# Second half-step of an inference layer: the fourth operand sum, the left-over products and two fetches take other places in the order

## The chip, the cores and the metric

The kernel runs on one core of a Trainium2 chip. The metric is device time in microseconds (us) of one execution; a run's figure is one such time, and the median of the runs is compared. TensorE (PE) does matmuls out of the on-chip memory into accumulation banks; VectorE (DVE) and ScalarE (ACT) do elementwise work; GpSimd (POOL) and SyncE (SP) here mostly issue DMAs. Each engine works through its own instructions in order.

## The reference

One layer of a diffusion trunk for 512 latent and 128 context tokens (640 columns in the kernel): a SwiGLU half-step, a mixing of tokens, and a second SwiGLU half-step. Cut to what matters here:

```python
def swiglu(h, w1, w3, w2):
    return (jax.nn.silu(h @ w1) * (h @ w3)) @ w2

# layer(...)
hh = rmsnorm(x, g[0]) * (1 + m[1]) + m[0]
x = x + 0.5 * m[2] * swiglu(hh, p['ffn1_w1'][l], p['ffn1_w3'][l], p['ffn1_w2'][l])
...
hh = rmsnorm(x, g[2]) * (1 + m[7]) + m[6]
x = x + 0.5 * m[8] * swiglu(hh, p['ffn2_w1'][l], p['ffn2_w3'][l], p['ffn2_w2'][l])
```

All data are f32; the width is 1024, the hidden width 2816, that is 11 blocks of 256. `m` is the modulation, a product of the conditioning vector with a 1024 x 9216 matrix.

## The kernel before

**Number format.** A matmul reads f32 rounded to a shorter form (fp32r). So each operand is split: ACT copies it into a high part, DVE subtracts that from the original and writes a low part. A product is three matmuls: high by high, high by low, low by high. PE reads a weight's low part at every third matmul.

**Seven products for eight.** A half-step halves the 1024 rows (or the 4 blocks of a group) and the 640 tokens, and multiplies by a scheme with seven block products instead of eight. It needs four sums of operand quarters (S1 to S4 in `operand_sums`, line 349) and sums of weight quarters. One `Granule` (line 243) is one 1024 x 256 piece of a weight matrix, loaded into one of two buffers `raw`. `parts` (line 256) splits two quarters and a half quarter of it into wB and wC, and then forms three weight sums in place in `raw`; `sums` (line 282) splits the result into `ww`, 128x2048. wB serves products A11 and A12, wC S4, `ww` S1, S3, A22 and S2. Each product is 12 matmuls of 128x320.

**The loop.** `products` (line 425) runs over a list of granules. In each it puts the products into three banks X, Y and Z in this order: A11 into X, S1 into Z, the left-over A22 and, after S2, the left-over S4 of the granule before (`tail`), A12 into X, S3 into Y. ACT copies X into Y behind A11, and Y into u2 behind S2 and into u3 behind S3. The weights of the next granule are prepared meanwhile.

**Where it is used.** The first half-step (`HalfStep` with `n_plain` 11) uses the scheme for its up-projection only; its down-projection multiplies plainly, with w2 split by `Whole.split` (line 294). Beside that, `modulation` (line 888) lets DVE work off the modulation's columns, two reductions each, with `columns.tile(hs.at_vec)`, where `at_vec` names the DVE instruction behind which they are to be placed. The second half-step (`run`, line 596) has 20 granules in the up-projection (w1 and w3 of blocks 1 to 10; block 0 is done plainly ahead), then a down-projection over three groups of blocks: blocks 0 to 2 plainly in four column groups, then blocks 3 to 6 and 7 to 10 in 4 + 4 granules (`last`). The gated values go to DRAM (`g_dram`) and come back by `fetch` (line 608) as the operands of the down-projection.

**What sets the order.** A scheduler simulates the program and orders each engine's instructions; matmuls keep the written order. `tc.issue_after(i)` says that what follows comes behind instruction i. In `products`, `next_parts(copied, gr.low)` places the next granule's `parts` behind the copy of X and behind the low part of this granule's `ww`. In the second half-step the first two granules are special: the operand sums S1 to S4 are written as one chain on DVE ahead of the loop, S4's terms and low parts last, and the second granule's `parts` come behind the low part of S2 (`behind=summed`). The loads of x from `x2_dram` that follow overwrite the operands' source.

**Fetches.** Most fetches are issued on SP between weight loads; those for which a buffer is freed late are issued on POOL. In `used(i)` (line 634) two of the third group's seven, A11 and S1, go out on POOL behind S3 of `last[1]`; their buffers were last read by the plain products.

Of the kernel before, what the change touches and what calls it, by code (L numbers as in the profile page):

```python
# [7 lines left out]
F32 = mybir.dt.float32  # L8
# [15 lines left out]
FB = F // 256  # L24
# [7 lines left out]
def tile_trunk(ctx: ExitStack, tc: tile.TileContext, a: dict):  # L32
# [210 lines left out]
    class Granule:  # L243
# [5 lines left out]
        def load(self):  # L249
            self.raw = rawp.tile([128, 2048], F32, tag="raw", name="raw")[:, : 512 * self.nk].rearrange("p (k n) -> p k n", n=256)  # L250
            return self.fetch(self.raw)
# [4 lines left out]
        def parts(self, fp, ties=()):  # L256
            ties = iter(ties)

            def tied(*args):
                with ExitStack() as st:  # L260
                    t = next(ties, None)
                    if t is not None:
                        st.enter_context(tc.issue_after(t.ins))
                    tt(vec, *args)
# [17 lines left out]
        def sums(self):  # L282
# [3 lines left out]
            act(t[0], flat, AF.Copy)  # L286
# [4 lines left out]
    class Whole(Granule):  # L291


        def split(self, fp=None):
# [8 lines left out]
            for (c0, c1, h), (_, _, lw) in zip(*t):  # L303
                act(h, flat[:, c0:c1], AF.Copy)
                tt(vec, lw, flat[:, c0:c1], h.bitcast(F32), ALU.subtract)
# [8 lines left out]
    class HalfStep:  # L314
# [34 lines left out]
        def operand_sums(self, pair):  # L349
# [30 lines left out]
            for f, i, r in (  # L380
                (terms, S1, 0), (terms, S1, 1), (terms, S3, 0), (low, S1, 0), (terms, S2, 0), (low, S1, 1), (terms, S3, 1),
                (terms, S2, 1), (low, S2, 0), (low, S2, 1), (low, S3, 0), (low, S3, 1), (terms, S4, 0), (terms, S4, 1),
            ):
                f(i, r)
                if (f, i) == (low, S2):
                    behind = prev.ins
            low(S4, 0)
            low(S4, 1)
            return behind
# [35 lines left out]
        def products(self, work, between, then=(), behind=None, prepared=False, first=()):  # L425
# [11 lines left out]
            for i, (gr, A, done, used) in enumerate(work):  # L437
# [25 lines left out]
                if self.n_plain < FB and i:  # L463
                    next_parts(copied, gr.low)
# [3 lines left out]
                if tail:  # L468
                    tail[0]()
# [74 lines left out]
        def run_whole(self, x, gate, final, between, behind, first):  # L544
# [32 lines left out]
            for q in G:  # L577
                last = q == G[-1]
                for j in range(4):
# [3 lines left out]
                    if m + 1 < len(down):  # L583
                        down[m + 1].split(self.fp if last and j < 2 else None)
                    for hf in range(1 if last and j else 2):
# [10 lines left out]
        def run(self, x, gate, final, behind=None, first_ties=()):  # L596
# [19 lines left out]
            def between(i, at):  # L616
                if (i, at) == (0, 1):
# [7 lines left out]
            def down_done(q, j):  # L625
# [8 lines left out]
                def used(i):  # L634
                    if (q, j, i) == (1, 1, S3):
                        fetch(2, A11, nc.gpsimd)
                        fetch(2, S1, nc.gpsimd)
# [91 lines left out]
    with ExitStack() as ph:  # L729
# [134 lines left out]
        hs.operand_sums(lambda r: x_all[:, 2 * r : 2 * r + 2, :])  # L864
# [1138 lines left out]
    summed = hs.operand_sums(lambda r: x_pairs[r])  # L2003
    for g in range(4):
        nc.sync.dma_start(out=x_pairs[g], in_=x2_dram[:, 2 * g : 2 * g + 2, :])
    hs.run(
        lambda: x, half_m[:, 1], lambda d, hf: nc.sync.dma_start(out=a["y"][:, d, half(hf)], in_=x[d][:, half(hf)]),
        behind=summed, first_ties=[normed_last] * 5,
# [129 lines left out]
```

## Time and profile before

| | us |
|---|---|
| median of 3 runs (lowest to highest) | 1847.83 (1846.72 to 1850.73) |
| the profiled execution, own time | 1846.77 |
| its span, first to last instruction | 1845.0 |
| ACT busy | 841.9 (46%) |
| DMA, mean rate | 162 GB/s |

How to read it: a group or timeline row has the line of the kernel, the engine, the operation, then output<-inputs by the program's tile names. L39 is the helper of every elementwise operation of two tensors, L52 that of every matmul, so tiles tell more than lines. `ps_f` is an accumulation bank of the half-steps, `S` and `hm` are operands (hm holds the quarters of the modulated input, later fetched ones), `x` the operand's source, `raw`, `wB`, `wC` and `ww` weights, `u` a copy of a bank, `s` a gate, `g` a split gated value, `op` a fetched operand. In the timeline the first number is the start, the second the time until the row's last instruction ends, and the bracket the idle time before it with what ended it. Neighbouring instructions of an engine overlap by some 0.08 us. The up-projection of the second half-step begins at about 1411 us, its down-projection at about 1692.

### The profile page before, as it was taken

How to read it: one execution, taken by the hardware profiler on the slowest of the kernel's cores; microseconds unless marked ns; L12 is line 12 of the kernel's file. 1: busy time of each engine (PE TensorE's matmuls, PEld its weight loads, DVE VectorE, ACT ScalarE, POOL GpSimd, SP SyncE). 2: the span in 40 equal slices, each digit the busy share in tenths (PEclk: the TensorE clock that was granted, in tenths of full speed). 3: DMA queues.
4: the chain of work that ended last, by engine and by line, in shares of the span. 5: the costliest groups of instructions: out<-in, count | busy, mean ns of one | idle time of the engine just before them, and what ended most of it. 6: DMA issues, size and time to landing. Idle time of an engine off the chain costs nothing.

```text
span 1845.0 us, 30710 instructions
## 1 busy us (share of the span) xinstructions
PE 1801.0 (98%) x12658; PEld 1767.9 (96%) x12658; DVE 1292.5 (70%) x2173; ACT 841.9 (46%) x1447; POOL 34.9 (2%) x61
## 2 busy tenths in 40 slices
PE   6999999999999999999999999999999899999989
PEld 4999999999999999999999989999999899999989
DVE  6888886575786667854754557787767778886576
ACT  6654454112654453543543455673336455554232
POOL 0000001110000000000000000000000000000000
PEclk9999999999999999999999999999999999999999
DMA  8345448863323233221222254675652445557952
GB/s 333 138 154 171 153 150 321 319 222 125 119 79 132 74 106 116 88 99 52 81 102 75 95 171 130 216 249 208 211 183 75 154 149 169 191 165 278 351 206 85
DMA packets 125709, 299.75 MB, mean 162 GB/s; under 512 B 9473, under 2 KB 88705, under 8 KB 112897
## 3 DMA queue, kind: packets, MB, share of 16 engines
q1 hardware_dynamic: 116242, 257.09, 40.5%
q0 software_dynamic: 9328, 40.71, 6.1%
q8 instruction: 99, 1.62, 0.4%
q14 instruction: 40, 0.33, 0.1%
HBM read 234.20 MB, written 63.63 MB: 161 GB/s over the span
## 4 chain that ended last, share of the span: by engine, by line
PE 89%; DMA 4%; DVE 4%; ACT 2%; issue 1%; SPq 0%; DVEq 0%; ACTq 0%
PE ps_f L52 44%; PE ps_p L52 23%; PE ps_t L52 11%; PE sc L52 2%; PE ps_o L52 2%; PE ps_n L52 2%; DMA ada<-csil_dram 2%; DMA P<-nm_dram 1%; PE ps_wT L55 1%; PE ps_qkT L55 1%; PE ps_u L52 1%; DVE junk L712 1%; DMA x<-in_x 1%; DMA raw_a<-in_w_ada_k 1%; DMA raw_a<-in_w_ada_c 0%
## 5 line engine op out<-in xcount | busy, mean ns | idle before, releaser
L52 PE MATMUL ps_f<-S,ww 128*128 128x320 f32 x1992 | 320.0, 311 | 5.6 <-ACT ww L286 3.8
L52 PEld LDWEIGHTS ps_f<-S,ww 128*128 128x128 f32 x1992 | 300.7, 189 | 6.1 <-ACT ww L286 4.1
L52 PE MATMUL ps_p<-hH,wH 128*128 128x320 f32 x864 | 273.5, 316 | 1.0 <-DVE C L42 1.0
L52 PE MATMUL ps_p<-hH,wL 128*128 128x320 f32 x864 | 267.0, 309 | 0.0
L52 PE MATMUL ps_p<-hL,wH 128*128 128x320 f32 x864 | 266.8, 309 | 0.0
L52 PE MATMUL ps_f<-hm,ww 128*128 128x320 f32 x1248 | 200.2, 313 | 7.6 <-ACT ww L286 4.1
L52 PEld LDWEIGHTS ps_f<-hm,ww 128*128 128x128 f32 x1248 | 189.7, 191 | 8.8 <-ACT ww L286 4.4
L52 PE MATMUL ps_t<-wH,hH 128*128 128x256 f32 x640 | 185.4, 290 | 0.0
L52 PE MATMUL ps_t<-wH,hL 128*128 128x256 f32 x640 | 181.9, 284 | 1.1 <-DVE hL L39 1.1
L52 PE MATMUL ps_t<-wL,hH 128*128 128x256 f32 x640 | 181.6, 284 | 0.0
L39 DVE TENSOR_TENSOR ww<-raw,ww 128x2048 fp32r<-128x2048 f32 (+1 forms) x62 | 138.7, 2238 | 40.4 <-ACT ww L286 26.4
L52 PEld LDWEIGHTS ps_p<-hH,wH 128*128 128x128 f32 x864 | 162.4, 188 | 1.9 <-DVE C L42 1.4
L52 PEld LDWEIGHTS ps_p<-hL,wH 128*128 128x128 f32 x864 | 162.5, 188 | 0.5
L52 PEld LDWEIGHTS ps_p<-hH,wL 128*128 128x128 f32 x864 | 162.2, 188 | 0.0
L52 PE MATMUL ps_f<-hm,wB 128*128 128x320 f32 x1008 | 161.5, 309 | 0.0
L52 PEld LDWEIGHTS ps_f<-hm,wB 128*128 128x128 f32 x1008 | 151.3, 188 | 0.0
L39 DVE TENSOR_TENSOR wL<-raw,wH 128x2048 fp32r<-128x2048 f32 x49 | 112.1, 2288 | 40.5 <-ACT wH L122 40.4
L122 ACT ACTIVATE wH<-raw 128x2048 fp32r<-128x2048 f32 x49 | 93.6, 1910 | 80.8 <-PE ps_p L52 76.7
L286 ACT ACTIVATE ww<-raw 128x2048 fp32r<-128x2048 f32 x48 | 91.8, 1913 | 73.4 <-DVE raw L39 55.0
L39 DVE TENSOR_TENSOR raw<-raw 128x1024 f32<-128x1024 f32 x144 | 124.2, 863 | 1.4
L52 PEld LDWEIGHTS ps_t<-wH,hL 128*128 128x128 f32 x640 | 123.1, 192 | 1.5 <-DVE hL L39 1.5
L52 PEld LDWEIGHTS ps_t<-wL,hH 128*128 128x128 f32 x640 | 123.3, 193 | 0.2
(299 smaller groups left out, 3207.6 us busy)
## 6 DMA issues: line engine op xcount, KB each, us to landing
g_dram<-g SPq DMA_DIRECT2D x44, 640.0 KB, 4.6
raw_a<-in_w_ada_c SPq DMA_DIRECT2D x32, 512.0 KB, 3.9
raw<-in_w1b SPq DMA_DIRECT2D x11, 1024.0 KB, 4.9
raw<-in_w3b SPq DMA_DIRECT2D x11, 1024.0 KB, 7.1
raw<-in_w1a SPq DMA_DIRECT2D x10, 1024.0 KB, 4.7
raw<-in_w3a SPq DMA_DIRECT2D x10, 1024.0 KB, 4.8
hm<-g_dram POOLq DMA_DIRECT2D x8, 1280.0 KB, 10.5
raw_a<-in_w_ada_k SPq DMA_DIRECT2D x8, 1024.0 KB, 11.3
```

What stands on the lines that cost most here:

```text
L39: return eng.tensor_tensor(out=out, in0=in0, in1=in1, op=op)
L52: tc.keep_in_program_order(nc.tensor.matmul(*args, **kw))
L55: tc.keep_in_program_order(nc.tensor.transpose(*args, **kw))
L122: act(h, raw, AF.Copy)
L286: act(t[0], flat, AF.Copy)
L712: vec.tensor_tensor_reduce(out=junk, in0=raw, in1=self.csil[:, v, :], op0=ALU.mult, op1=ALU.add, scale=1.0, scalar=0.0, accum_out=mod[:, c ...
```

## The change

Five edits. (1) `operand_sums` no longer issues S4's terms and low parts itself, but gives back a function `last` that does; in the second half-step `run` calls it when the loop reaches its first granule, behind the last weight sum of the second granule, and the four x reloads follow it (`rest`). The first half-step calls it at once. (2) `next_parts` places the third and later granules' `parts` also behind ACT's high part of the current granule's `ww` (`gr.high`). (3) In the second granule of the up-projection the left-over A22 product comes ahead of S1. (4) The two fetches of `used(i)` go from POOL to SP, behind the load of `last[3]`. (5) In the first half-step's down-projection the modulation's reductions at the head of each step are placed behind the low part of the next w2 piece.

```diff
         def load(self):
...
-            return self.fetch(self.raw)
+            self.loaded = self.fetch(self.raw)
+            return self.loaded
...
-                    tt(vec, *args)
+                    self.at_vec = tt(vec, *args)
...
-            act(t[0], flat, AF.Copy)
+            self.high = act(t[0], flat, AF.Copy)
...
-                tt(vec, lw, flat[:, c0:c1], h.bitcast(F32), ALU.subtract)
+                self.low = tt(vec, lw, flat[:, c0:c1], h.bitcast(F32), ALU.subtract)
...
-                (terms, S2, 1), (low, S2, 0), (low, S2, 1), (low, S3, 0), (low, S3, 1), (terms, S4, 0), (terms, S4, 1),
+                (terms, S2, 1), (low, S2, 0), (low, S2, 1), (low, S3, 0), (low, S3, 1),
             ):
                 f(i, r)
-                if (f, i) == (low, S2):
-                    behind = prev.ins
-            low(S4, 0)
-            low(S4, 1)
-            return behind
+            behind = prev.ins
+
+            def last(ins=None):
+                nonlocal prev
+                prev = ins or prev
+                for f in (terms, low):
+                    for r in range(2):
+                        f(S4, r)
+
+            return behind, last
...
                 if self.n_plain < FB and i:
-                    next_parts(copied, gr.low)
+                    next_parts(copied, gr.low, gr.high)
+                early = tail and self.n_plain < FB and i == 1 and not prepared
+                if early:
+                    tail[0]()
                 into(Z, S1, True)
...
-                if tail:
+                if tail and not early:
                     tail[0]()
...
                         down[m + 1].split(self.fp if last and j < 2 else None)
+                        self.at_vec = down[m + 1].low
...
             def between(i, at):
+                if (i, at) == (0, 0):
+                    rest(work[1][0].at_vec)
...
                     if (q, j, i) == (1, 1, S3):
-                        fetch(2, A11, nc.gpsimd)
-                        fetch(2, S1, nc.gpsimd)
+                        with tc.issue_after(last[3][0].loaded):
+                            fetch(2, A11)
+                            fetch(2, S1)
...
-    summed = hs.operand_sums(lambda r: x_pairs[r])
-    for g in range(4):
-        nc.sync.dma_start(out=x_pairs[g], in_=x2_dram[:, 2 * g : 2 * g + 2, :])
+    summed, fourth = hs.operand_sums(lambda r: x_pairs[r])
+
+    def rest(ins):
+        fourth(ins)
+        for g in range(4):
+            nc.sync.dma_start(out=x_pairs[g], in_=x2_dram[:, 2 * g : 2 * g + 2, :])
```

What this does to the engines' orders is shown at three places. The numbers behind the names tell buffers apart; lines are those of each version.

**The second granule's weights on DVE and ACT** (raw_15053; x_14306 and x_14307 receive S4's terms, hm_14342 its split form). DVE before:

```order
L39 TENSOR_TENSOR S_15163<-x_13738,S_15163 128x640
L39 TENSOR_TENSOR x_14306<-x_14306,x_13737 128x2x320
L39 TENSOR_TENSOR x_14307<-x_14307,x_13738 128x2x320
L39 TENSOR_TENSOR wB_15210<-raw_15053,wB_15209 128x1024
L39 TENSOR_TENSOR wC_15212<-raw_15053,wC_15211 128x512
L39 TENSOR_TENSOR hm_14342<-x_14306,hm_14342 128x640
L39 TENSOR_TENSOR hm_14342<-x_14307,hm_14342 128x640
L39 TENSOR_TENSOR raw_15053<-raw_15053 128x2x4x128
L39 TENSOR_TENSOR s_15299<-ps_f_15222,u_15297 128x320
L39 TENSOR_TENSOR raw_15053<-raw_15053 128x4x128 x2
L39 TENSOR_TENSOR ww_15249<-raw_15053,ww_15248 128x2048
```

DVE now, at the same place:

```order
L39 TENSOR_TENSOR S_15163<-x_13738,S_15163 128x640
L39 TENSOR_TENSOR wB_15200<-raw_15053,wB_15199 128x1024
L39 TENSOR_TENSOR wC_15202<-raw_15053,wC_15201 128x512
L39 TENSOR_TENSOR raw_15053<-raw_15053 128x2x4x128
L39 TENSOR_TENSOR raw_15053<-raw_15053 128x4x128 x2
L39 TENSOR_TENSOR x_14306<-x_14306,x_13737 128x2x320
L39 TENSOR_TENSOR x_14307<-x_14307,x_13738 128x2x320
L39 TENSOR_TENSOR ww_15249<-raw_15053,ww_15248 128x2048
L39 TENSOR_TENSOR g_15280<-SO_14892,g_15280 128x1280
L39 TENSOR_TENSOR s_15299<-ps_f_15222,u_15297 128x320
L39 TENSOR_TENSOR hm_14342<-x_14306,hm_14342 128x640
L39 TENSOR_TENSOR hm_14342<-x_14307,hm_14342 128x640
```

The four instructions of S4 moved behind the weight sums, its low parts even behind `ww_15249`. ACT before, from the copy u3 of the first granule on (wB_15320 and ww_15357 are the third granule's):

```order
L422 ACTIVATE u_15297<-ps_f_15221 128x320
L516 ACTIVATE s_15299<-s_15299 128x320
L462 ACTIVATE ps_f_15305<-ps_f_15304 128x320
L271 ACTIVATE wB_15320<-raw_15207 128x1024
L271 ACTIVATE wC_15322<-raw_15207 128x512
L286 ACTIVATE ww_15248<-raw_15053 128x2048
L286 ACTIVATE ww_15357<-raw_15207 128x2048
L516 ACTIVATE s_15355<-ps_f_15221 128x320
L422 ACTIVATE u_15373<-ps_f_15305 128x320
L516 ACTIVATE s_15387<-s_15387 128x320
L422 ACTIVATE u_15416<-ps_f_15305 128x320
```

ACT now, from the second granule's high part on:

```order
L287 ACTIVATE ww_15248<-raw_15053 128x2048
L428 ACTIVATE u_15297<-ps_f_15221 128x320
L374 ACTIVATE hm_14342<-x_14306 128x640
L374 ACTIVATE hm_14342<-x_14307 128x640
L468 ACTIVATE ps_f_15305<-ps_f_15304 128x320
L272 ACTIVATE wB_15320<-raw_15197 128x1024
```

The high part moved ahead of u3, of the copy of X and of the third granule's wB and wC.

**The third granule's weights on ACT**, the rows that follow (raw_15197 was raw_15207 before; u_15373 and u_15416 are the second granule's u2 and u3):

```order
L272 ACTIVATE wC_15322<-raw_15197 128x512
L525 ACTIVATE s_15343<-ps_f_15221 128x320
L525 ACTIVATE s_15299<-s_15299 128x320
L428 ACTIVATE u_15373<-ps_f_15305 128x320
L525 ACTIVATE s_15387<-s_15387 128x320
L428 ACTIVATE u_15416<-ps_f_15305 128x320
L287 ACTIVATE ww_15357<-raw_15197 128x2048
L468 ACTIVATE ps_f_15424<-ps_f_15423 128x320
```

`ww_15357` stood right behind `ww_15248`; it now stands behind u_15416. From the fourth granule on `ww` stands ahead of the u3 of the granule before it, then and now.

**The third of the last eight granules on ACT** (raw_18088; raw_18168 is the fourth). Before, from the copy of X of the second on:

```order
L462 ACTIVATE ps_f_18172<-ps_f_18171 128x320
L422 ACTIVATE u_18240<-ps_f_18172 128x320
L271 ACTIVATE wB_18187<-raw_18088 128x1024
L271 ACTIVATE wC_18189<-raw_18088 128x512
L422 ACTIVATE u_18284<-ps_f_18172 128x320
L462 ACTIVATE ps_f_18294<-ps_f_18293 128x320
L271 ACTIVATE wB_18309<-raw_18168 128x1024
L271 ACTIVATE wC_18311<-raw_18168 128x512
L286 ACTIVATE ww_18224<-raw_18088 128x2048
```

Now:

```order
L468 ACTIVATE ps_f_18172<-ps_f_18171 128x320
L272 ACTIVATE wB_18187<-raw_18088 128x1024
L272 ACTIVATE wC_18189<-raw_18088 128x512
L428 ACTIVATE u_18240<-ps_f_18172 128x320
L287 ACTIVATE ww_18224<-raw_18088 128x2048
L428 ACTIVATE u_18284<-ps_f_18172 128x320
L468 ACTIVATE ps_f_18294<-ps_f_18293 128x320
```

wB and wC moved ahead of the copy u2, and `ww_18224` ahead of u3 and of the fourth granule's wB and wC. On SP the two moved fetches now stand between the loads of raw_18168 and raw_18290.

More of the change, by code (lines that the diff above doesn't have):

```diff
@@ L594, in run_whole, with run @@
                     unit(G[-1], j, f, 1)
-        def run(self, x, gate, final, behind=None, first_ties=()):
+        def run(self, x, gate, final, behind=None, first_ties=(), rest=None):
             def nothing(*args):
@@ L863, in tile_trunk @@
         hs.gate_plain(1, 1, ps)
-        hs.operand_sums(lambda r: x_all[:, 2 * r : 2 * r + 2, :])
+        hs.operand_sums(lambda r: x_all[:, 2 * r : 2 * r + 2, :])[1]()
         x_stack.close()
@@ L2002, in tile_trunk @@
         hs.gate_plain(f, 1, (ps[f, 0], ps[f, 1]))
-    summed = hs.operand_sums(lambda r: x_pairs[r])
-    for g in range(4):
-        nc.sync.dma_start(out=x_pairs[g], in_=x2_dram[:, 2 * g : 2 * g + 2, :])
+    summed, fourth = hs.operand_sums(lambda r: x_pairs[r])
[3 more added lines that the diff above has]
+            nc.sync.dma_start(out=x_pairs[g], in_=x2_dram[:, 2 * g : 2 * g + 2, :])
     hs.run(
         lambda: x, half_m[:, 1], lambda d, hf: nc.sync.dma_start(out=a["y"][:, d, half(hf)], in_=x[d][:, half(hf)]),
-        behind=summed, first_ties=[normed_last] * 5,
+        behind=summed, first_ties=[normed_last] * 5, rest=rest,
     )
```

## The prediction

> **What bounds the kernel now.** First the page's busy times, then the list of what TensorE (PE) waited for, then its timeline where it waited.
>
> ```profile
> PE 1801.0 (98%) x12658; PEld 1767.9 (96%) x12658; DVE 1292.5 (70%) x2173; ACT 841.9 (46%) x1447; POOL 34.9 (2%) x61
> ...
> PE ps_f L52 <- ACT ww L286: 8.0, 2, 4.1
> PE ps_f L52 <- DVE ww L39: 5.3, 3, 2.1
> ```
>
> PE is the bound: a change that moves work between other engines pays only where PE stands still. For `ps_f`, the half-steps' products, it waits five times for `ww`, the split weights (total, times, longest). The timeline (start, us, then the instructions) has them in three places.
>
> ```profile
> 339.05 2.21 PE L52 MATMUL ps_f<-hm,ww 128*128 128x320 f32 x14
> 343.34 2.40 PE L52 MATMUL ps_f<-hm,ww 128*128 128x320 f32 x10 [2.08 <-DVE ww L39]
> 345.54 2.82 PE L52 MATMUL ps_f<-S,ww 128*128 128x320 f32 x12
> 348.20 1.92 PE L52 MATMUL ps_f<-hm,ww 128*128 128x320 f32 x12
> ...
> 1446.52 1.92 PE L52 MATMUL ps_f<-hm,wB 128*128 128x320 f32 x12
> 1452.28 0.55 PE L52 MATMUL ps_f<-S,ww 128*128 128x320 f32 x2 [3.85 <-ACT ww L286]
> 1454.61 3.04 PE L52 MATMUL ps_f<-S,ww 128*128 128x320 f32 x10 [1.77 <-DVE ww L39]
> ...
> 1460.49 1.92 PE L52 MATMUL ps_f<-S,ww 128*128 128x320 f32 x12
> ...
> 1754.40 1.92 PE L52 MATMUL ps_f<-op,ww 128*128 128x320 f32 x12
> 1756.16 1.92 PE L52 MATMUL ps_f<-S,wB 128*128 128x320 f32 x12
> 1762.21 0.90 PE L52 MATMUL ps_f<-hm,ww 128*128 128x320 f32 x2 [4.13 <-ACT ww L286]
> 1764.54 6.57 PE L52 MATMUL ps_f<-hm,ww 128*128 128x320 f32 x34 [1.42 <-DVE ww L39]
> 1770.94 1.92 PE L52 MATMUL ps_f<-S,wC 128*128 128x320 f32 x12
> ```
>
> Unhindered, 12 matmuls take 1756.16 - 1754.40 = 1.76 us, so each place's loss can be counted. Place A (1446 to 1460): 36 matmuls lie between 1446.52 and 1460.49, 13.97 us instead of 5.28: **8.69 lost**. Place B (1756 to 1771): 48 matmuls in 14.78 us instead of 7.04: **7.74 lost**. Place C (340): 36 matmuls from 339.05 to 348.20, 9.15 instead of 5.28: 3.87 lost. All are more than the waits listed, because the granted clock (last but two of each row) drops behind them:
>
> ```profile
> 344.20:347.60 3.40, 3.40 (x14) 3.40 (x14) 3.40 (x9) 0.00 (x0) 0.76 (x2) 0.51 0.93 298
> ...
> 1453.50:1457.00 3.50, 2.39 (x9) 2.39 (x10) 3.50 (x3) 0.00 (x0) 0.00 (x0) 0.50 0.37 108
> ```
>
> Behind the single 2.08 us wait of place C, 22 matmuls took 348.20 - 343.34 = 4.86 us instead of 3.23: the clock cost 1.6.
>
> **Place A: the second granule's weights.** PE waits for the high part of `ww_15248`, then for its low part. Before, on ACT and DVE:
>
> ```profile
> 1444.95 0.44 ACT L516 ACTIVATE s<-ps_f 128x320 f32<-128x320 f32 x1 [0.70 <-PE ps_f L52]
> ...
> 1448.87 1.05 ACT L271 ACTIVATE wB<-raw 128x1024 fp32r<-128x1024 f32 x1
> ...
> 1450.34 1.90 ACT L286 ACTIVATE ww<-raw 128x2048 fp32r<-128x2048 f32 x1
> ...
> 1438.87 2.29 DVE L39 TENSOR_TENSOR S<-x,S 128x640 fp32r<-128x640 f32 x3
> 1441.08 1.55 DVE L39 TENSOR_TENSOR x<-x 128x640 f32<-128x640 f32 x2
> 1442.55 1.22 DVE L39 TENSOR_TENSOR wB<-raw,wB 128x1024 fp32r<-128x1024 f32 x1
> ...
> 1444.29 1.55 DVE L39 TENSOR_TENSOR hm<-x,hm 128x640 fp32r<-128x640 f32 x2
> ...
> 1452.26 2.29 DVE L39 TENSOR_TENSOR ww<-raw,ww 128x2048 fp32r<-128x2048 f32 x1 [3.27 <-ACT ww L286]
> 1454.47 1.49 DVE L39 TENSOR_TENSOR g<-SO,g 128x1280 fp32r<-128x1280 f32 x1
> ...
> 1457.61 2.67 DVE L39 TENSOR_TENSOR raw<-raw 128x1024 f32<-128x1024 f32 x3
> ```
>
> With the new order DVE goes from 1441.08 straight to wB and wC (1444.29 - 1442.55 = 1.74) and the three weight sums (2.67): done at 1445.5, three and a half us earlier. The fourth sum's terms follow (1.47, to 1446.9). ACT is free of its silu at 1445.4, so the high part runs 1445.5 to 1447.4: it no longer stands behind the third granule's wB and wC. The low part is done at 1447.4 + 2.3 = 1449.7. On PE the left-over A22 product of the first granule now follows 1446.52's twelve: 1448.28 to 1450.04, at no cost, as it moves ahead of S1 instead of behind it. A22 writes on Y, whose copy u now stands behind the high part on ACT and ends at 1447.8: 0.5 to spare. S1 starts at 1450.04 and reads the low part at its third matmul, 1450.33: 0.6 to spare. The stall of place A goes.
>
> What comes late next? The fourth sum's low parts now stand behind `ww` low, g (1.49) and an add of about 0.5: 1449.7 + 1.4 + 0.4 + 1.5 = 1453.0. PE's S4 product follows A22, S1 and S2, at 1453.56: hidden by 0.6, and beyond that a us costs a us. The x reloads (four DMAs on SP) start at 1446.9 instead of 1441.9; behind them SP holds the fourth granule's load, whose raw buffer frees at 1449.7 anyway. x is read again only in the down-projection. Nothing.
>
> The **new wait** is at the third granule. Its high part `ww_15357` stood directly behind `ww_15248` on ACT; now it stands behind `u_15416`, the copy of Y that ACT may make only when PE has ended S3. Such a copy starts 0.26 behind PE and takes 0.44:
>
> ```profile
> 1467.78 0.44 ACT L422 ACTIVATE u<-ps_f 128x320 f32<-128x320 f32 x1 [2.05 <-PE ps_f L52]
> ```
>
> S3 of the second granule ends at 1458.84 (seven products from 1446.52 on, 1.76 each), so u runs 1459.1 to 1459.5, the high part 1459.4 to 1461.3, the low part to 1463.7. PE ends A11 of the third granule at 1460.60, reads the high part at once and the low part at 1460.89: it waits 0.7, does two matmuls, and waits to 1463.7. Loss **2.8**. The ends of this cost: nothing if ACT and DVE were faster than these rows (the orders exclude a gain), 8.69 as at place A if the clock stays low for two windows. Nearest is place C, the same wait for a low part: 2.8 + 1.6 for the clock = **4.4**. From the fourth granule on the high part stands ahead of the u copy again, with 3 us to spare.
>
> The clock is where a page weighs against a row. The Trainium skill, "TensorE: Matmul & The Clock Gate", section "HAM oscillation — how this bites in real kernels", has the rule that PE gaps up to about 3.4 us do no harm. The rows at 343.34 and 344.20 speak against it: 2.08 us of waiting, clock 0.51. By the rule the new wait costs 2.8, not 4.4.
>
> Place A: 8.69 - 4.4 = **4.3 gained**.
>
> **Place B: the third granule of the last eight.**
>
> ```profile
> 1734.19 0.70 POOL L610 DMA_DIRECT2D S<-g_dram  x1 [3.24 <-PE ps_f L52]
> 1735.50 0.71 POOL L610 DMA_DIRECT2D hm<-g_dram  x1 [0.62 <-PE ps_f L52]
> ...
> 1736.22 55.40 SPq L74 DMA_DIRECT2D raw<-in_w2b  x10
> ...
> q0 software_dynamic: 668, 3.26, 100.5%
> ...
> raw<-in_w2b SPq DMA_DIRECT2D x2, 512.0 KB, 12.3
> ...
> 1745.80 0.42 ACT L462 ACTIVATE ps_f<-ps_f 128x320 f32<-128x320 f32 x1 [1.32 <-PE ps_f L52]
> ...
> 1751.08 0.44 ACT L422 ACTIVATE u<-ps_f 128x320 f32<-128x320 f32 x1 [4.86 <-PE ps_f L52]
> 1751.41 1.05 ACT L271 ACTIVATE wB<-raw 128x1024 fp32r<-128x1024 f32 x1
> ...
> 1754.60 0.55 DVE L42 SCALAR_TENSOR_TENSOR x<-ps_f,half_m,x 128x320 f32<-128x320 f32 x1 [0.68 <-PE ps_f L52]
> ```
>
> The two POOL fetches of 1.31 MB are issued just ahead of this granule's weights, and from 1732 to 1740 POOL's queue q0 moves 3.26 MB and fills the DMA engines. The weights land 12.3 us after their issue, at 1748.5. And ACT has their wB behind u, which PE releases at 1751.08. With the change the fetches stand on SP behind the next granule's load, which waits for a raw buffer until 1745. About 2.6 MB less lie ahead: at 3.26 MB in 8 us that is 6.4 us, so landing by about 1742. ACT now has wB ahead of u: right behind the copy at 1745.80, that is at 1746.2. Then by the durations above: wB 1.05, DVE 1.74 and 2.67 with a residual (0.7) between, 1752.4; high part to 1754.3; low part behind the residual at 1754.60, 1755.1 to 1757.4. PE needs the high part at 1757.92 and the low part at 1758.2: ready. **7.74 gained**. If the landing moved only to 1749, the low part would come about 1.5 us late.
>
> **The modulation.** In the first half-step three reductions move behind the low part of w2.
>
> ```profile
> 314.40 2.29 DVE L39 TENSOR_TENSOR ww<-raw,ww 128x2048 fp32r<-128x2048 f32 x1 [0.17 <-ACT ww L304]
> ```
>
> The first of these low parts already waited for ACT there, so the reduction ahead of it cost it nothing. At the other two PE runs without a gap, and the low part that place C waits for keeps its place. Bounds: 0 and, if place C went too, a gain of 3.87. I take 0.
>
> **Sum.** 1846.8 (the profiled execution, span 1845.0) - 4.3 - 7.7 = 1834.8. Its time lies 1.1 below the median of 1847.83, so I forecast **1835**.
>
> **Rivals.**
> 1. The clock stays full behind the new wait, which two matmuls split into 0.7 and 2.0 us: 1846.8 - 5.9 - 7.7 = 1833.2. Against it stands place C, for it that each part is no longer than C's 2.08. The rule above would have it so.
> 2. No new wait at the third granule: 1846.8 - 8.7 - 7.7 = 1830.4. It would need ACT to copy Y before PE is done with it.
> 3. Place B remains: the weights were late for another reason than the two fetches: 1842.5. For it: ACT was itself behind u. Against it: wB is now ahead of u.
> 4. The fourth sum is late, or the second granule's low part, by some 2 us with the clock behind it: about 1838.
> 5. **Slower.** SP serves in order, and the fifth of the last eight granules has its load behind the two fetches. One such fetch on SP took long under full load:
>
> ```profile
> S<-g_dram SPq DMA_DIRECT2D x1, 1280.0 KB, 14.6
> ```
>
> If two ran one after the other at that price from 1746 on, and the weights 12.3 behind them, these would land at 1787.5. ACT wants them after the X copy one granule earlier, at 1770.4: 17 us of waiting, and 1846.8 - 12 + 17 + 1.6 = 1853. It decides from a landing at about 1782 on. Against it: behind 1750 little else is on the DMA engines.
> 6. The stalls only move (the change doesn't do what it says): 1846.8.
>
> **Chances.** Forecast 0.45, rivals 1 to 6: 0.25, 0.08, 0.11, 0.05, 0.04, 0.02. The range is 1830 to 1841: it holds all but 3, 5 and 6. A measurement of this kernel tells about 0.2% (3.7 us) from no change; below 1844 lie the forecast and rivals 1 to 4: faster 0.93, same 0.03, slower 0.04.
>
> **What would show it.** In the profile after: no wait for `ww` between the first and second granule of the up-projection, with the A22 product (hm,ww) ahead of S1; a wait of 0.7 and 2 us at the third granule's S1 and a clock near 0.5 behind it; wB of the third of the last granules directly behind the X copy, and 36 matmuls without a wait there; place C as before. The sum is wrong if the S4 product waits for DVE, if the third granule's wait is under 1 or over 4 us, or if the weights of the fifth of the last granules land late.

## The result, and the profile after

| | before | after |
|---|---|---|
| median (lowest to highest), us | 1847.83 (1846.72 to 1850.73) | 1836.81 (1836.16 to 1838.36) |
| ratio of the runs, 95% interval | | 0.9942 (0.9927 to 0.9956) |
| profiled execution: own time, span, us | 1846.77, 1845.0 | 1836.16, 1834.4 |

The change gains 11.0 us by the medians, 10.6 by the profiled executions. Forecast were 1835 with a range of 1830 to 1841.

PE's waits for weights in the changed kernel (total, times, longest), which answer to the 8.0 and 5.3 us of before:

```profile
PE ps_f L52 <- DVE ww L39: 4.7, 3, 2.0
...
PE ps_f L52 <- ACT ww L287: 0.6, 1, 0.6
```

Four waits are left. One is place C, unchanged (2.0). The others are in PE's timeline of the changed kernel; first place A, from the second granule's A11 to the third's left-over A22:

```profile
1447.34 1.92 PE L52 MATMUL ps_f<-hm,wB 128*128 128x320 f32 x12
1449.10 1.92 PE L52 MATMUL ps_f<-hm,ww 128*128 128x320 f32 x12
1450.86 3.68 PE L52 MATMUL ps_f<-S,ww 128*128 128x320 f32 x24
...
1459.66 1.92 PE L52 MATMUL ps_f<-hm,wB 128*128 128x320 f32 x12
1462.21 0.55 PE L52 MATMUL ps_f<-S,ww 128*128 128x320 f32 x2 [0.63 <-ACT ww L287]
1464.54 1.73 PE L52 MATMUL ps_f<-S,ww 128*128 128x320 f32 x10 [1.77 <-DVE ww L39]
1466.11 1.92 PE L52 MATMUL ps_f<-hm,ww 128*128 128x320 f32 x12
```

The second granule's S1 follows A22 without a gap, as forecast. The new wait stands at the third granule, 0.63 and 1.77 us: 24 matmuls take 1466.11 - 1459.66 = 6.45 us instead of 3.52, so 2.93 are lost where 2.8 were forecast. The clock did not drop behind it (ten matmuls in 1.73). Place A gained 8.69 - 2.93 = 5.76.

Place B in the changed kernel: PE from the copy of X of the third granule on, and ACT and DVE ahead of it:

```profile
1751.26 1.92 PE L52 MATMUL ps_f<-S,wB 128*128 128x320 f32 x12
1753.02 5.44 PE L52 MATMUL ps_f<-hm,ww 128*128 128x320 f32 x36
...
1740.90 0.42 ACT L468 ACTIVATE ps_f<-ps_f 128x320 f32<-128x320 f32 x1 [1.32 <-PE ps_f L52]
1741.23 1.05 ACT L272 ACTIVATE wB<-raw 128x1024 fp32r<-128x1024 f32 x1
...
1750.17 2.28 DVE L39 TENSOR_TENSOR ww<-raw,ww 128x2048 fp32r<-128x2048 f32 x1
```

No wait: all 7.74 are gained. The weights landed 5.7 us after their issue instead of 12.3. The low part ends at 1752.45 and is wanted at 1753.3.

A wait that the prediction did not have, called **place D** from here on, at the seventh of the last eight granules. First PE, then ACT, whose wB for this granule waits for its load (the runs below ask whether that is the cause):

```profile
1802.30 0.46 PE L52 MATMUL ps_f<-hm,ww 128*128 128x320 f32 x2
1803.70 1.73 PE L52 MATMUL ps_f<-hm,ww 128*128 128x320 f32 x10 [0.94 <-DVE ww L39]
1805.26 1.92 PE L52 MATMUL ps_f<-op,ww 128*128 128x320 f32 x12
...
1791.86 1.06 ACT L272 ACTIVATE wB<-raw 128x1024 fp32r<-128x1024 f32 x1 [1.26 <-DMA raw<-in_w2b]
```

Twelve matmuls take 2.96 us instead of 1.76: 1.20 lost. So between the second granule's A11 and PE's last products 5.76 + 7.74 - 1.20 = 12.3 us were gained (12.0 forecast). Two small differences take 1.7 back. The changed kernel reaches place A 0.82 later (1447.34 against 1446.52). And the span ends 6.26 us behind the start of PE's last twelve matmuls instead of 5.42. That leaves the 10.6. The start of the last twelve matmuls, before and after:

```profile
1839.58 1.92 PE L52 MATMUL ps_f<-op,ww 128*128 128x320 f32 x12
```

```profile
1828.14 1.92 PE L52 MATMUL ps_f<-op,ww 128*128 128x320 f32 x12
```

### The profile page after: what moved, and what is told of

The parts are those of the page before. It is cut to its first block, busy times and chain, and to the rows that moved or that the text cites. A ratio compares the mean times of both kernels' runs of the same rounds, so it can differ in the third digit from the quotient of the medians.

```text
span 1834.4 us, 30708 instructions
## 1 busy us (share of the span) xinstructions
PE 1796.2 (98%) x12658; PEld 1763.7 (96%) x12658; DVE 1291.7 (70%) x2173; ACT 841.4 (46%) x1447; POOL 33.4 (2%) x59
## 4 chain that ended last, share of the span: by engine, by line
PE 89%; DMA 5%; DVE 4%; ACT 2%; issue 1%; SPq 0%; DVEq 0%; ACTq 0%
PE ps_f L52 44%; PE ps_p L52 23%; PE ps_t L52 11%; PE sc L52 2%; PE ps_o L52 2%; DMA ada<-csil_dram 2%; PE ps_n L52 1%; PE ps_wT L55 1%; PE ps_qkT L55 1%; PE ps_u L52 1%; DMA P<-nm_dram 1%; DMA raw_a<-in_w_ada_c 1%; DVE junk L725 1%; DMA x<-in_x 1%; DMA raw_a<-in_w_ada_k 1%
## 5 line engine op out<-in xcount | busy, mean ns | idle before, releaser
L52 PEld LDWEIGHTS ps_t<-wH,hH 128*128 128x128 f32 x640 | 123.2, 192 | 0.2
```

Source lines behind the costliest of these rows:

```text
L52: tc.keep_in_program_order(nc.tensor.matmul(*args, **kw))
```

## The experiments

To be free of what differs ahead of place A, the table counts from the start of the second granule's A11 to the start of PE's last twelve matmuls, in each kernel's profile ("A to end"). "Rest" is the span from there on. Ratios are against runs of the kernel before on the same chip; the kernel before had medians from 1845.39 to 1848.97 on these chips, so medians from different chips can't be compared to within a few us. Each "A to end" is one execution. Many of the ratios' intervals overlap; differences of 1 or 2 us below are read from the waits in the profiles, not from the medians.

| kernel | A to end | rest | median | ratio (95%) |
|---|---|---|---|---|
| before | 393.06 | 5.42 | 1847.83 | |
| changed | 380.80 | 6.26 | 1836.81 | 0.9942 (0.9927 to 0.9956) |
| only_fetches | 386.18 | 6.24 | 1842.14 | 0.9964 (0.9953 to 0.9975) |
| without_fetches | 388.99 | 5.40 | 1844.83 | 0.9978 (0.9967 to 0.9988) |
| without_modulation | 382.30 | 6.22 | 1836.76 | 0.9935 (0.9917 to 0.9953) |
| no_early | 379.42 | 6.15 | 1835.72 | 0.9927 (0.9909 to 0.9944) |
| fourth_in_chain | 383.71 | 6.28 | 1836.52 | 0.9945 (0.9924 to 0.9967) |
| high_first | 379.81 | 6.29 | 1833.78 | 0.9921 (0.9906 to 0.9936) |
| g_later | 378.05 | 6.22 | 1830.44 | 0.9905 (0.9890 to 0.9920) |
| s4_behind_load | 381.07 | 6.15 | 1836.36 | 0.9933 (0.9911 to 0.9955) |
| parts_behind_u2 | 386.96 | 6.26 | 1840.61 | 0.9961 (0.9948 to 0.9974) |
| pool_new_order | 383.07 | 5.41 | 1834.95 | 0.9940 (0.9922 to 0.9958) |
| both_repairs | 376.84 | 6.14 | 1830.58 | 0.9916 (0.9898 to 0.9935) |
| pool_order_g_later | 377.75 | 5.41 | 1833.04 | 0.9920 (0.9906 to 0.9933) |

**The parts one by one.** First edit (4) alone on the kernel before:

```diff
-            return self.fetch(self.raw)
+            self.loaded = self.fetch(self.raw)
+            return self.loaded
...
-                        fetch(2, A11, nc.gpsimd)
-                        fetch(2, S1, nc.gpsimd)
+                        with tc.issue_after(last[3][0].loaded):
+                            fetch(2, A11)
+                            fetch(2, S1)
```

> The kernel before with edit (4) alone: the two fetches go to SP behind the load of the fourth of the last eight granules. My theory: place B goes (7.7 us), place A stays at 8.7, and place D, the wait that is new near the end, comes with it (1.2), because it follows from the stall of place B being gone: 1846.8 - 7.7 + 1.2 = 1840.3 us. Rival 1: place D comes from edits (1) to (3): it is absent here, 1839.1. Rival 2: the weights at place B are late for another reason than the two fetches: 1846.8.

PE's waits for weights from place A on, then ACT's wB at place B and at place D:

```profile
1454.75 0.59 PE L52 MATMUL ps_f<-S,ww 128*128 128x320 f32 x2 [3.85 <-ACT ww L287]
1457.08 3.03 PE L52 MATMUL ps_f<-S,ww 128*128 128x320 f32 x10 [1.74 <-DVE ww L39]
...
1810.72 1.73 PE L52 MATMUL ps_f<-hm,ww 128*128 128x320 f32 x10 [0.94 <-DVE ww L39]
...
1748.25 1.05 ACT L272 ACTIVATE wB<-raw 128x1024 fp32r<-128x1024 f32 x1
...
1797.53 1.05 ACT L272 ACTIVATE wB<-raw 128x1024 fp32r<-128x1024 f32 x1
```

Place A is there, place B is gone, and place D is there without edits (1) to (3): it comes with edit (4). From A to end 6.9 us are gained. ACT's order at place B is the changed kernel's, with wB directly behind the copy of X (1747.92 to 1748.34). At place D ACT waits for no load here, and PE still waits 0.94.

The reverse, the changed kernel with edit (4) undone:

> The changed kernel with edit (4) undone: the two fetches on POOL again. My theory: place A stays as in the changed kernel (one wait of 0.6 and 1.8 us at the third granule, 2.9 lost), place B is back with 7.7 lost, place D is gone: 1836.2 + 7.7 - 1.2 = 1842.7 us. Rival: the parts of the change depend on each other (fetches alone or the order alone suffice at place B): about 1836.

Place B is back with its 4.13 and 1.42, place D is gone. A to end is 8.2 longer: 8.0 at place B, 1.4 for a clock that dropped at the third granule, less 1.2 at place D. But for that clock the two parts of the change add up: 6.9 + 4.1 + 1.4 = 12.4, and 12.3 together.

Edit (5) undone (the line `self.at_vec = down[m + 1].low` taken out):

> The changed kernel with edit (5) undone: the modulation's reductions in the first half-step's down-projection stand where they stood before. My theory: nothing changes, 1836.2 us, within 1 us of the changed kernel, and place C keeps its wait of 2 us and its loss of 3.9. Rival 1: the 0.8 us by which the changed kernel reaches place A later than the kernel before comes from this edit: 1835.4, and place A begins at 1446.5. Rival 2: the edit gains something in the first half-step that other differences hide: above 1837.

Nothing changed: a median of 1836.76 against 1836.81, place C with 2.00. This kernel reached place A at 1446.38, which looks like rival 1; but the other kernels with edit (5), all the same up to the operand sums, reached it anywhere from 1443.70 to 1450.14. The 0.8 us are within what differs from run to run.

Behind the same wait as in the changed kernel this one shows a lower clock. Six profiled kernels have this wait of 0.63 and 1.77 us. The time from the third granule's A11 to its left-over S4 is 9.97 in two of them (the changed kernel, parts_behind_u2), 11.35 to 11.39 in three (without_fetches, without_modulation, s4_behind_load) and 12.74 in one (pool_new_order): the drop costs 0, 1.4 or 2.8 us for one and the same wait. The Trainium skill, "TensorE: Matmul & The Clock Gate", section "HAM oscillation — how this bites in real kernels", has the rule "no PE-idle gaps >~3.4µs"; taken as a limit below which a gap does no harm, four of these six profiles disagree. The Trainium skill, on the same page, section "What's actually happening", has the activity window run free. The clock records bear that out.

Within each of the fourteen profiles the changes of the granted clock up to the last products lie whole multiples of 3.413 us apart, to 0.002 us: in without_modulation the clock is low from 343.68, 729.38 and 1463.25 us on, which is 113 and 215 times 3.413 apart. Cut at these moments, the time around the wait looks so in the changed kernel, in without_modulation and in pool_new_order (start and end, length, PE's busy time and matmuls, granted clock, DMA share, GB/s):

```profile
1459.94:1463.35 3.41, 2.20 (x14) 1.00 0.06 23
1463.35:1466.77 3.42, 2.23 (x15) 1.00 0.30 79
```

```profile
1459.84:1463.25 3.41, 1.35 (x8) 1.00 0.00 0
1463.25:1466.66 3.41, 3.08 (x11) 0.50 0.56 190
```

```profile
1456.85:1460.26 3.41, 1.67 (x10) 1.00 0.02 6
1460.26:1463.68 3.42, 2.77 (x10) 0.50 0.48 141
1463.68:1467.09 3.41, 3.41 (x14) 0.50 0.40 166
```

What differs is where the 2.4 us of waiting fall. Where at most 1.21 or 1.38 us of them lie in one such stretch (the two kernels with 9.97), the clock stays; where 1.74 to 2.17 lie in one (the other four), the next stretch runs at half the clock, in pool_new_order the next two. No sharp limit comes out of it: in high_first 1.70 us here and 1.85 at place C lay in one stretch, and the clock stayed. No run shifted the wait alone.

**Place A: what the fourth sum and the early product do.** Edit (3) undone, the left-over A22 behind S1 again:

```diff
-                early = tail and self.n_plain < FB and i == 1 and not prepared
+                early = tail and False
```

> The changed kernel with edit (3) undone: in the second granule the left-over A22 product stands behind S1 again. By the changed kernel's trace S1 would start at 1449.1 and want the low part at 1449.4, which comes at 1450.6: 1.2 us lost there. But without edit (3) the third granule's high part stands ahead of the copy u3 of the second on ACT, so it is ready about 1.4 us sooner against a PE that is 1.2 us later: the wait of 2.9 us at the third granule all but goes (0.1 to 0.4 left). My theory: 1836.2 + 1.2 - 2.6 = 1834.8 us, so edit (3) by itself costs time. Rival 1: edit (3) is needed and the wait at the third granule stays: 1837.4. Rival 2: the clock drops behind the 1.2 us wait: 1836.4.

PE at the second granule's S1, then ACT at the third granule, in this kernel:

```profile
1450.13 1.73 PE L52 MATMUL ps_f<-S,ww 128*128 128x320 f32 x10 [1.09 <-DVE ww L39]
...
1458.36 1.92 ACT L287 ACTIVATE ww<-raw 128x2048 fp32r<-128x2048 f32 x1
1460.76 0.44 ACT L428 ACTIVATE u<-ps_f 128x320 f32<-128x320 f32 x1 [0.48 <-PE ps_f L52]
```

A wait of 1.09 at the second granule, none at the third, where the high part stands ahead of u3 again: 1.4 us less than with edit (3) in two profiles whose clock did not drop there. The ratios (0.9927 and 0.9942) can't tell the two kernels apart.

Edit (1) undone, the fourth sum in the chain again:

```diff
-            behind = prev.ins
+                if (f, i) == (low, S2):
+                    behind = prev.ins
...
+    fourth()
+    for g in range(4):
+        nc.sync.dma_start(out=x_pairs[g], in_=x2_dram[:, 2 * g : 2 * g + 2, :])
...
     def rest(ins):
-        fourth(ins)
-        for g in range(4):
-            nc.sync.dma_start(out=x_pairs[g], in_=x2_dram[:, 2 * g : 2 * g + 2, :])
+        pass
```

> The changed kernel with edit (1) undone: S4's terms and low parts stand in the chain ahead of the loop again, the x reloads behind them, and the second granule's weights behind the low part of S2. By rows: S4's 3.0 us of DVE delay the second granule's weight sums to 1448.6; the high part runs 1448.9 to 1450.8, the low part to 1453.1, against PE asking at 1450.0: waits of 0.8 and 2.0, 2.8 us lost; the third granule's high part stands ahead of u2 and u3 and is ready in time. Theory: place A loses 2.8 there instead of 2.9 at the third granule, so edit (1) by itself gains nothing: 1836.8 as a median, 1.4 more if the clock drops. Rival: the second granule's wait goes back to 3.9 and 1.8 us, 1840 or above.

Its waits, at the second granule:

```profile
1450.79 0.56 PE L52 MATMUL ps_f<-S,ww 128*128 128x320 f32 x2 [0.80 <-ACT ww L287]
1453.12 6.17 PE L52 MATMUL ps_f<-S,ww 128*128 128x320 f32 x22 [1.77 <-DVE ww L39]
```

0.80 and 1.77 at the second granule instead of 0.63 and 1.77 at the third; the 2.9 us that this kernel is longer from A to end are nearly all the clock (22 matmuls in 6.17), twice the drop that was allowed for. So edit (1), with edit (3) in place, only moved this wait by one granule. Edit (2) was not run: without it every engine has the same order.

**The new wait.** One tie more, u3 of the second granule behind the third's high part:

```diff
-                u3 = copy_of(Y, "nry")
+                with ExitStack() as st:
+                    if i == 1 and self.n_plain < FB and not prepared:
+                        st.enter_context(tc.issue_after(work[i + 1][0].high.ins))
+                    u3 = copy_of(Y, "nry")
```

> The changed kernel with one tie more: the copy u3 of the second granule is placed behind the high part of the third granule's weights on ACT. Theory 1 (the new wait comes from the order on ACT alone, as the prediction had it): the high part starts when u3 did or earlier, and the wait of 2.9 us shrinks to below 1 us. Theory 2 (DVE is the limit, whose last weight sum ended at 1459.2 in the changed kernel, only 0.7 before u3 did its work at 1459.9): high part 1459.3 to 1461.2, low part to 1463.4, so 1.8 us of the 2.9 stay, in one wait for the low part; a gain of 1.1 us, 1835.7 as a median, without a drop of the clock.

ACT and PE of this kernel:

```profile
1455.65 1.91 ACT L287 ACTIVATE ww<-raw 128x2048 fp32r<-128x2048 f32 x1 [1.59 <-DVE raw L39]
...
1459.94 1.73 PE L52 MATMUL ps_f<-S,ww 128*128 128x320 f32 x10 [1.70 <-DVE ww L39]
```

The high part now waits for the weight sums on DVE, and 1.70 of PE's wait stays: theory 2 (from A to end 1.0 us is gained). Then what keeps DVE, the split g, put behind these sums:

```diff
+                if self.n_plain < FB and i == 1 and not prepared:
+                    between(i, 2)
...
-                if (i, at) == (0, 1):
-                    with tc.issue_after(work[1][0].low.ins):
+                if (i, at) == (1, 2):
+                    with tc.issue_after(work[2][0].at_vec.ins):
                         self.store_g(first, 0)
```

> The changed kernel with the split of block 0's gated values (g, 1.5 us of DVE at 1450.5) placed behind the last weight sum of the third granule; with that the high part of the third granule also comes ahead of the copy u3 on ACT. Theory 2 (DVE's queue behind the second granule's low part is the limit): weight sums done at 1457.3, high part to 1459.2, low part to 1461.4, wanted at 1461.7: the wait at the third granule goes, 2.9 us gained, 1833.9 as a median of runs in which the clock does not drop. Theory 1 (ACT's order alone): no better than the kernel with the tie on u3. Rival: g and the product that writes SO come late for the store or the banks, and a wait of over 1 us comes up at the third or fourth granule.

```profile
1454.91 1.92 ACT L287 ACTIVATE ww<-raw 128x2048 fp32r<-128x2048 f32 x1
...
1458.81 2.13 PE L52 MATMUL ps_f<-S,ww 128*128 128x320 f32 x12
```

The wait is gone but for 0.2 (twelve matmuls in 2.13 instead of 1.92), and the clock has nothing to drop behind: 2.75 us from A to end. The high part stands ahead of u3 here too, so the 2.75 are both orders together; g moved without that was not run.

**Place B: the landing or the order?** First the fetches as in the changed kernel, but on ACT the split of the third granule behind u2, as before:

```diff
-            act(t, p, AF.Copy)
+            self.copied = act(t, p, AF.Copy)
...
+                late = prepared and i == 1
-                if self.n_plain < FB and i:
+                if self.n_plain < FB and i and not late:
                     next_parts(copied, gr.low, gr.high)
...
-                if not last:
+                if not last and not late:
                     work[i + 1][0].sums()
...
                 u2 = copy_of(Y, "nacc" if i < 2 * FB - 2 else "nsq", 2)
+                if late:
+                    next_parts(self.copied)
+                    work[i + 1][0].sums()
```

> The changed kernel with place B's old order on ACT: the split of the third of the last eight granules is written behind the copy u2 of the second, which puts its high part behind u3 and the next copy of X, as it was before; the fetches stay on SP. It tells apart what at place B was the late landing and what the order. Theory 1 (landing alone): the weights are there, nothing is lost, 1836.8 as a median. Theory 2 (the order alone): all of the 7.7 us comes back, 1844. Theory 3 (both, the price of the order by the changed kernel's rows: high part behind the copy of X at 1753.3, so 1753.6 to 1755.5, low part to 1757.8, against PE asking at 1753.0): waits of 2.5 and 2 us, 4.5 lost, 1.6 more if the clock drops: 1841.3 to 1842.9.

```profile
1753.56 1.90 ACT L287 ACTIVATE ww<-raw 128x2048 fp32r<-128x2048 f32 x1
...
1755.51 0.57 PE L52 MATMUL ps_f<-hm,ww 128*128 128x320 f32 x2 [2.32 <-ACT ww L287]
1757.84 7.93 PE L52 MATMUL ps_f<-hm,ww 128*128 128x320 f32 x34 [1.76 <-DVE ww L39]
```

Nothing here waits for a DMA, and still the order costs 2.32 and 1.76 us of waiting, near theory 3's 2.5 and 2, and the clock more than was forecast (34 matmuls in 7.93; 5.25 in the next kernel). 48 matmuls take 14.33 us instead of 7.04: 7.3 lost, against 7.74 in the kernel before. That the two are so near is partly chance. The waits are 1.5 us shorter than the 4.13 and 1.42 of before, mainly because the fourth granule's wB and wC, which stood ahead of the high part on ACT, stand behind it here; the clock makes up for it. Place D is gone. The opposite case, the fetches on POOL (as in without_fetches) and the landing late, but the order held by ties:

```diff
-                copied = act(Y, X, AF.Copy)
+                with ExitStack() as st:
+                    if prepared and i == 2:
+                        st.enter_context(tc.issue_after(gr.high.ins))
+                    copied = act(Y, X, AF.Copy)
...
-                u2 = copy_of(Y, "nacc" if i < 2 * FB - 2 else "nsq", 2)
+                with ExitStack() as st:
+                    if prepared and i == 1:
+                        st.enter_context(tc.issue_after(work[i + 1][0].at_act.ins))
+                    u2 = copy_of(Y, "nacc" if i < 2 * FB - 2 else "nsq", 2)
...
-                u3 = copy_of(Y, "nry")
+                with ExitStack() as st:
+                    if prepared and i == 1:
+                        st.enter_context(tc.issue_after(work[i + 1][0].high.ins))
+                    u3 = copy_of(Y, "nry")
...
```

(`at_act` is the ACT copy into wC. The additions to x of that granule are placed behind the weight sums in the same way.)

> The changed kernel with the two fetches on POOL again, ahead of the load of the third of the last eight granules, so that this load lands late as before; but ties hold the orders of ACT and DVE around that granule's weights as the changed kernel has them (wB and wC ahead of u2, the high part ahead of u3, the weight sums ahead of the additions to x). It tells apart whether the fetches cost time at place B through the late landing or through the order that the scheduler made of it. Theory 1 (the order): the load of 1731.3 lands 12.3 us later, at 1743.6, wB follows at once, weight sums to 1748.2, high part to 1750.2, low part to 1752.5, wanted at 1753.3: no wait at place B, and 1836.8 us as a median, or 1.2 less if place D goes with it. Theory 2 (the landing): the 7.3 to 7.7 us come back, 1844.

```profile
1743.17 1.06 ACT L272 ACTIVATE wB<-raw 128x1024 fp32r<-128x1024 f32 x1 [2.54 <-DMA raw<-in_w2b]
...
1753.07 5.25 PE L52 MATMUL ps_f<-hm,ww 128*128 128x320 f32 x34 [0.27 <-DVE ww L39]
```

Now ACT does wait for the landing, 12.0 us behind the issue as before, and PE waits 0.27. That is theory 1, and with the run before it shows that place B was the order. Its 2.3 us from A to end above the changed kernel are mainly the clock at the third granule (2.8) and this wait, less place D, which this kernel does not have.

**Place D.** The last of POOL's five fetches goes behind the seventh granule's load:

```diff
-                    elif q == 1 and j == 3 and i in moves:
+                    elif q == 1 and j == 3 and i in moves and i != S3:
                         fetch(2, moves[i], nc.gpsimd)
+                    elif (q, j, i) == (2, 0, A11):
+                        with tc.issue_after(last[6][0].loaded):
+                            fetch(2, S4)
```

> The changed kernel with one fetch moved: the last of the five fetches on POOL, the third group's S4 operand (1.31 MB), goes to SP behind the load of the seventh of the last eight granules. Theory (place D is that load waiting its turn behind five fetches and the sixth granule's load: 8.6 MB from 1764.8 on): 1.31 MB less lie ahead, 3.2 us at 0.41 MB per us, so the load lands before ACT asks for it at 1790.6; the 1.2 us wait at place D goes, 1835.6 as a median. The fetch lands at about 1792, wanted at 1795. Rival 1: the load is slow by itself, the wait stays, 1836.8. Rival 2: the fetch on SP comes late and the product that reads it waits, 1837 or above.

From issue to landing (shortest, median, longest) of that load's two DMAs, in the changed kernel and in this one:

```profile
DMA to landing us min/median/max: 12.4/13.3/14.2
```

```profile
DMA to landing us min/median/max: 9.1/9.6/10.1
```

Four us sooner, and no wait at place D. That the time is the changed kernel's is the clock at the third granule (+1.4). But this does not show that the late landing was the cause, as the theory had it. PE's wait at place D is 0.94 or 0.95 us in all seven profiles that have it, whether ACT waited for the load (1.26 us in the changed kernel, 0.43 in fourth_in_chain) or not at all (only_fetches, without_modulation, no_early, high_first). What these seven share, and none of the other seven has, is DVE's order behind the seventh granule's wB. In the changed kernel:

```profile
1797.22 0.49 DVE L39 TENSOR_TENSOR t<-ps_f,u 128x320 f32<-128x320 f32 x1 [0.72 <-PE ps_f L52]
1797.63 0.68 DVE L39 TENSOR_TENSOR raw<-raw 128x512 f32<-128x512 f32 x1
...
1798.69 0.68 DVE L39 TENSOR_TENSOR raw<-raw 128x512 f32<-128x512 f32 x1
```

And in the kernel with the fetch moved:

```profile
1795.88 1.41 DVE L39 TENSOR_TENSOR raw<-raw 128x512 f32<-128x512 f32 x2
1798.04 0.49 DVE L39 TENSOR_TENSOR t<-ps_f,u 128x320 f32<-128x320 f32 x1 [0.75 <-PE ps_f L52]
```

Two of the three weight sums stand behind t (a sum of a bank and a copy u), which has to wait for PE, and an addition to x stands between them; in the other kernels both stand ahead of t. From there the chain goes on to the high part, the low part and PE. So place D is an order like place B, and moving the fetch changed that order along with the landing. No run holds the order and moves the landing alone. Both repairs together:

> The changed kernel with both repairs: g behind the third granule's weight sums, and the third group's S4 fetch on SP behind the load of the seventh granule. If the two waits are independent: from the second granule's A11 to the end of PE's work 380.8 - 2.75 - 1.2 = 376.9 us, and 1829.2 us as a median. Rival: without the wait at the third granule everything behind it comes earlier against the DMAs, and place D stays: 1830.4.

376.84 from A to end, as the sum had it; the list of PE's waits names weights at place C only. By the medians (1830.58, beside g_later's 1830.44 on another chip) the 1.2 us of place D can't be told.

Why this order appeared is not shown. It goes with the distance between the sixth granule's load on SP and the first of POOL's five fetches: 4.95 us before (1773.50 to 1778.45) and 1.24 after (1764.80 to 1766.04). While PE stood still at place B, the weights of the granules behind were prepared, their raw buffers came free, and the loads ran ahead. The last kernel has neither stall:

> The kernel with the fetches on POOL and the changed kernel's order held by ties, and beside it the split g behind the third granule's weight sums. It asks two things of a kernel without a stall at either place. First, place D: if it comes from the short distance between the sixth granule's load and the first fetch of the next five (1.2 us in the changed kernel, 5.0 in the kernel before, 2.4 in the kernel with the fetches on POOL and the new order), it stays away here, and from the second granule's A11 to the last product it takes 380.8 - 2.75 - 1.2 + 0.3 = 377.1 us; if it follows from the stalls being gone, 378.3. Second, the end: behind the start of PE's last twelve matmuls the span goes on for 6.1 to 6.3 us in every kernel with the two fetches on SP and for 5.4 in every one with them on POOL; if that is the fetches' doing, 5.4 here, else 6.2. The median: 1830, no different from the kernel with both repairs.

Place D stays away although no stall is left, the distance is 2.6 us (1764.12 to 1766.76), and the end takes 5.41. It has 0.65 above the 377.1, and PE's wait at place B is 0.57 here. The median, 1833.04, is 3 above the forecast; its ratio, 0.9920, does not differ from the 0.9916 of both_repairs. So the removed stall is not by itself what makes place D. A distance of 1.24 with five fetches behind it goes with place D in seven kernels, one of 2.3 to 5.2 without it in five, and with four fetches behind 1.24 it is absent in two; the distance was not changed alone.

## Why the prediction was right, and where it was not

- **Place A, the size:** forecast 4.3 gained, measured 5.76. The wait was sized 0.7 and 2.0 and came as 0.63 and 1.77; 2.8 lost, 2.93 measured. The mis-sized term is the clock, 1.6 us, which is 0 in the profiled execution. The runs show 0, 1.4 or 2.8 for the same wait, on average (0 + 0 + 1.4 + 1.4 + 1.4 + 2.8) / 6 = 1.2: the forecast and rival 1 are two outcomes of the same wait. Which of them comes follows from where the wait falls between the moments at which the clock can change, and that the prediction could not know.
- **Place A, the cause:** the prediction put the new wait on the place of u3 ahead of the high part. The tie on u3 alone gained 1.0 of it; with g out of DVE's way as well it was 2.75. The step that failed is that ACT's order alone sets the wait: DVE, whose weight sums end at 1459.2, was nearly as late. And "at no cost" for the early A22 was wrong: without it the profile is 1.4 us shorter, since the wait of 1.1 at the second granule is cheaper than the one that takes its place.
- **Place B:** 7.74 forecast and measured. But the step "the weights land 12.3 us after their issue" was not what cost the time. With the landing at 12.0 and the new order PE waits 0.27; with the landing early and most of the old order 7.3 us are lost. The fetches cost time through the order of ACT and DVE: moving them alone (only_fetches) changed it and took the wait away. That the scheduler reckons with a late landing there is my reading of it, not shown. The row that showed it was there: wB at 1751.41 followed u directly and waited for no DMA.
- **Modulation:** 0, as forecast.
- **What was missing:** place D, 1.2 us. Rival 5 looked for a load that lands late, at the fifth granule and behind the two moved fetches. At the seventh a load did land late, behind five fetches that the change didn't touch, but PE's wait there is that of DVE's order. The margins of S4 (0.6) and of the u copy held.
- **The end of the span:** 0.7 to 0.9 us longer in all ten kernels with the two fetches on SP (6.14 to 6.29) than in the four with them on POOL (5.40 to 5.42). PE, DVE and the last stores stand alike in both. The difference lies in ten semaphore instructions with which SP closes the program. The last store lands at about 1844.0 before and 1832.6 after. Ahead of that landing and behind it (how many; shortest, median and longest in ns; first and last start), before:

```profile
L2115 SPq EVENT_SEMAPHORE  x8: 17/28/28, 1842.6 to 1843.0; - x8
...
L2115 SPq EVENT_SEMAPHORE  x2: 28/28/28, 1844.0 to 1844.1; - x2
```

  and after:

```profile
L2132 SPq EVENT_SEMAPHORE  x2: 17/22/28, 1831.2 to 1831.2; - x2
...
L2132 SPq EVENT_SEMAPHORE  x8: 28/28/28, 1832.6 to 1833.1; - x8
```

  Eight then two in all four kernels with the fetches on POOL, two then eight in the eight with two fetches more on SP, three then seven in the two with three more. The six that come behind the landing instead of ahead of it take 0.4 us; what makes the other 0.4 (a drain behind them starts 0.3 later and lasts 0.13 instead of 0.01) stays open. It belongs to edit (4), whose gain by the profiles is 7.74 - 1.20 - 0.84 = 5.7 us.
- **The sum** came out 1.4 below the profiled time, and the forecast 1.8 below the median: place A gained 1.5 more, but there was nothing in it for place D (1.2), for the end (0.8) and for the difference ahead of place A (0.8, from run to run). That it came so near is in part luck: a clock that happened to stay up set off losses that nobody had forecast.

## What to carry to other kernels

Moving a transfer can cost or gain time through the order that a scheduler makes of it, not through the landing. Look whether the row behind it names the DMA as what it waited for, and even then whether the wait that counts stands in another kernel where it doesn't: at place D ACT waited 1.26 us for a load in one kernel and not at all in others, and PE waited 0.94 in all of them. And when a wait moves on by one granule, look for the engine that is full just there (here DVE, by one 1.5 us split that could wait) before reordering the engine that shows the wait.

## What the runs showed that was not expected

- The granted clock fell behind one and the same wait of 0.63 and 1.77 us in four of six profiles, for 3.41 or 6.83 us (a cost of 1.4 or 2.8 us), and not at all in the other two. It changed only at moments whole multiples of 3.413 us apart. g_later, which has no such wait there, has its four runs within 1830.0 to 1831.2.
- The same 0.8 us at the end of the program come with two more DMAs on SP, though the last store lands equally far behind the last products.
- The two DMAs of one load, 0.5 MB each, took 12.4 to 14.2 us to land with five fetches of 1.31 MB ahead of it, and 9.1 to 10.1 with four.
